# Moving the products of the first half's fourth expert block behind the second half's routing, in a one-layer hybrid decoder

## The chip, the cores and the metric

The kernel runs on one core of one Trainium2 chip. The metric is the device time of one execution in microseconds (us). Three runs of the kernel before took 4314.97, 4318.94 and 4319.62 us; their median, 4318.94 us, is the time before.

## What is computed

One layer on 1024 tokens of width 1024. Three sequence mixers (mLSTM, SSD, forgetting attention) share a normalised input; their outputs are gated, summed and projected with `w_out`. Then comes a product-key expert layer (PEER), and last a gated per-layer embedding and a final norm. The change touches the expert layer:

```
def peer(h, w_q, keys1, keys2, u, v):
    q = (hf @ w_q).astype(f32).reshape(t, PEER_HEADS, 2, PEER_QDIM // 2)
    ...
    v1, i1 = lax.top_k(s1, PEER_TOPK)
    v2, i2 = lax.top_k(s2, PEER_TOPK)
    ...
    gates = jax.nn.softmax(top_s, axis=-1).astype(h.dtype)
    def block(args):
        xb, ib, gb = args
        act = jax.nn.gelu(jnp.einsum('td,thkd->thk', xb, u[ib]), approximate=False)
        return jnp.einsum('thk,thkd->td', act * gb, v[ib])
```

There are 16384 experts, each one row of 1024 fp32 numbers in `u` and one in `v`. Each token picks 8 heads x 16 = 128 experts. For a block of 128 tokens the first `einsum` needs 128 gathers of 128 rows each (one row for each token, 4 KB a row, 512 KB a gather) and 128 row-by-row scalar products.

## The kernel before

The 1024 tokens are worked in two halves of 512, and each half has four blocks of 128 tokens (`tb`). The order of the program is: mixers of half 0, its routing keys (`route_keys`), mixers of half 1 with half 0's routing beside them, then the expert layer, then the embedding.

**Gathers and dots.** `experts_in` (lines 1018 to 1033) handles the first `einsum` of one block. It loads the block's token vectors into the tile `hft`, and for each of the 128 slots `rows` (line 1004) takes a row buffer, POOL issues an indirect DMA into it (line 1014), and VectorE (DVE) multiplies the gathered rows with `hft` and adds along the row (line 1027, in two rows of the trace: the product, named CUSTOM_DVE_ANT_0, and a short read of the accumulator). This document calls the DVE instruction of line 1027 a dot. After the 128th dot ScalarE (ACT) applies the gelu (line 1030) and DVE multiplies with the gates (line 1031).

**Row buffers.** `rows` takes the buffers in turn. `UB = 3` buffers have the tag `ug` in a pool that lives through the program; the argument `extra` adds more. Before the change all four blocks of half 0 get two more, `ug0` and `ug1`, from the mixers' pool (`mx`, in the code `pool["s"]`), so five. A gather into a buffer has to wait until the dot that read its earlier content is done.

**Who decides the order.** Outside of `experts_out` a scheduler of the framework sets each engine's order of instructions: what the program emits earlier goes first where both are ready by its own estimate, and each engine then executes its list strictly in order. The dots of half 0 are emitted after the mixers of half 1 (lines 1341 to 1343) and the scheduler spreads them among those mixers' work.

**What follows the dots.** `mx` is closed (line 1344), and its memory goes to the pool `v1`, with a wait for each tile that overlaps an old one. `scatter` (lines 1059 to 1108) builds one-hot matrices on DVE (lines 1091 and 1103), which PE multiplies in bf16 (line 1070), so that the second `einsum` of three blocks becomes a dense matmul with all of `v`. Its first chunk, for the blocks 0 to 2 of half 0, runs beside `mixer_out(1)`, the projection with `w_out` (lines 876 to 887; its DVE addition is line 884). `route_keys(1)` then starts with a norm: a sum of squares (line 310) and the reciprocal of the root (line 287 is its first DVE row). The routing of half 1 (`route(r1)`, lines 1356 and 1357) is next, and then `experts_out`, where the order on DVE is as written, not scheduled.

Other lines that are named below: 810 normalises the SSD mixer's output, with its statistics in the small operations from line 265 to 226; 840 and 841 combine a branch projection with its gate; 183 makes the low part of a split weight; 205 is an fp32 matmul of a projection; 1347 makes the scatter's `iota` tile, the first DVE row of the scatter.

Of the kernel before, what the change touches and what calls it, by code (L numbers as in the profile page):

```python
# [26 lines left out]
NC = T // P  # L27
# [29 lines left out]
def tile_trunk(ctx, tc, xT, pT, w_in, w_tm, w_br, w_q, keys, peer_u, peer_v,  # L57
# [5 lines left out]
    up = ctx.enter_context(tc.tile_pool(name="up", bufs=1))  # L63
# [10 lines left out]
    def st(shape, dt=F32, tag="t", bufs=1, pool_=None):  # L74
        p = pool_ or pool["r" if tag in ("mg", "rw", "keyt") or tag.startswith("p_") else "s"]
        return p.tile(list(shape), dt, tag=tag, name=nm(tag), bufs=bufs)
# [778 lines left out]
    def mixer(hf, H, columns, side=iter(()), then=None):  # L855
        cd = mg = out = None
        for b, mix in ((2, fox), (0, mlstm), (1, ssd)):
            Y = [ytile() for _ in range(KT)]
            Z = None if hf else halves()
            gs, gate = gates(b, H)  # L860
            if cd is None:
                cd = mix(hf, H, Y, Z, columns, side)
                mg = st([P, KT, T], tag="mg")
                if then is not None:
                    then()
            else:
                mix(hf, H, Y, Z, *cd, gate)
            if b == 1 and hf == 0:
                a = st([P, 4, T], F32R, tag="v8")
                bs = [st([P, 2, T], F32R, tag=f"ug{i}") for i in range(2)]  # L870
                out = [a[:, k] for k in range(4)] + [b_[:, k] for b_ in bs for k in range(2)], []
                out[1].extend(live(dt=F32R) for _ in range(KT))
            branch(gs, gate, b, Z or Y, mg, out)
        return out or mg
# [15 lines left out]
    def top16(src, val, ind, w):  # L890
        V.max(out=val[:, 0:8], in_=src)
        V.max_index(out=ind[:, 0:8], in_max=val[:, 0:8], in_values=src)
        V.match_replace(out=w, in_to_replace=val[:, 0:8], in_values=src, imm_value=-3e38)
        V.max(out=val[:, 8:16], in_=w)
        V.max_index(out=ind[:, 8:16], in_max=val[:, 8:16], in_values=w)
# [35 lines left out]
    def pick(pos, d, ge, gm, starts):  # L931

        V.tensor_tensor(out=ge, in0=pos.unsqueeze(2).to_broadcast([P, 8, 16, 16]),
                        in1=starts.unsqueeze(1).to_broadcast([P, 8, 16, 16]), op=ALU.is_ge)
        o = []
        for x in d:
            V.tensor_tensor(out=gm, in0=ge, in1=x, op=ALU.mult)
            V.tensor_tensor(out=gm[:, :, 0:8], in0=gm[:, :, 0:8], in1=gm[:, :, 8:16], op=ALU.add)
            r = st([P, 8, 16], BF, tag="p_pk", bufs=2 * NC + 1)
            with nc.allow_low_precision(reason="sums of small integers, exact"):  # L940
                V.tensor_reduce(out=r, in_=gm[:, :, 0:8].rearrange("p h a k -> p h k a"), axis=AX.X, op=ALU.add)
            o.append(r)
        return o

    def route(res, tv, ti, ge, gm):

        spare, cs = ge, gm[:, 0:8 * NCAND].rearrange("p (h n) -> p h n", h=8)
        ge, gm = (t.bitcast(BF).rearrange("p (h a k) -> p h a k", h=8, a=16) for t in (ge, gm))
        for tb in range(NC):

            iv = st([P, 16, 17], BF, tag="p_iv")
            V.memset(iv[:, :, 0:1], 0.0)
            V.tensor_copy(out=iv[:, :, 1:17], in_=ti[:, tb])
            dv = st([P, 8, 2, 16], BF, tag="p_dv")
            V.tensor_tensor(out=dv.rearrange("p a b c -> p (a b) c"), in0=iv[:, :, 1:17], in1=iv[:, :, 0:16],
                            op=ALU.subtract)
            vv = tv[:, tb].rearrange("p (a b) c -> p a b c", b=2)
            c0 = 0
            for a, n in CAND:
                V.tensor_tensor(out=cs[:, :, c0:c0 + n], in0=vv[:, :, 1, 0:n],  # L960
                                in1=vv[:, :, 0, a:a + 1].to_broadcast([P, 8, n]), op=ALU.add)
                c0 += n
            V.tensor_tensor(out=cs[:, :, c0:c0 + 8], in0=vv[:, :, 0, 8:16],
                            in1=vv[:, :, 1, 0:1].to_broadcast([P, 8, 8]), op=ALU.add)
            tsc = st([P, 8, 16], tag="p_ts")
            pos = st([P, 8, 16], U32, tag="p_pos")
            for h in range(8):
                top16(cs[:, h, :], tsc[:, h, :], pos[:, h, :], spare[:, h * P:h * P + NCAND])
            posb = st([P, 8, 16], BF, tag="p_pb", bufs=2)
            V.tensor_copy(out=posb, in_=pos)  # L970

            d1 = dv[:, :, 0, :].unsqueeze(3).to_broadcast([P, 8, 16, 16])
            f1, sa = pick(posb, (d1, dst_.unsqueeze(1).to_broadcast([P, 8, 16, 16])), ge, gm, sta)
            bb = st([P, 8, 16], BF, tag="p_pb", bufs=2)
            V.tensor_tensor(out=bb, in0=posb, in1=sa, op=ALU.subtract)
            i1f = f1.rearrange("p h k -> p (h k)")
            d2 = dv[:, :, 1, :].unsqueeze(3).to_broadcast([P, 8, 16, 16])
            f2, = pick(bb, (d2,), ge, gm, stb)
            ii = st([P, P], I32, tag="ii", bufs=NC + 1, pool_=up)
            V.scalar_tensor_tensor(out=ii, in0=i1f, scalar=128.0, in1=f2.rearrange("p h k -> p (h k)"),  # L980
                                   op0=ALU.mult, op1=ALU.add)
            gt = st([P, 8, 16], tag="gt", bufs=2 * NC, pool_=up)
            V.tensor_tensor(out=gt, in0=tsc, in1=tsc[:, :, 0:1].to_broadcast([P, 8, 16]), op=ALU.subtract)
            A.activation(out=gt, in_=gt, func=AF.Exp)
            gsum = st([P, 8], tag="p_gs", bufs=2)
            V.tensor_reduce(out=gsum, in_=gt, axis=AX.X, op=ALU.add)
            V.reciprocal(out=gsum, in_=gsum)
            V.tensor_tensor(out=gt, in0=gt, in1=gsum.unsqueeze(2).to_broadcast([P, 8, 16]), op=ALU.mult)
            res.append([gt, ii, i1f, f2.rearrange("p h k -> p (h k)")])
            yield  # L990

    def route_slots(res, pj=pg):

        for r in res:
            tp = pj((P, 2, P))
            for i in range(2):
                PE.matmul(tp[:, i], lhsT=r[2 + i], rhs=identb, start=True, stop=True)
                t = st([P, P], BF, tag="i12", bufs=4 * NC, pool_=up)
                A.copy(out=t, in_=tp[:, i])
                r[2 + i] = t  # L1000
# [3 lines left out]
    def rows(table, ii, extra):  # L1004

        for s in range(P):
            while True:
                turn["u"] = (turn["u"] + 1) % (len(extra) + UB)
                m = turn["u"]
                p, tag = (up, "ug") if m < UB else extra[m - UB]  # L1010
                if tag not in lent:
                    break
            x = st([P, D], tag=tag, bufs=UB if m < UB else 1, pool_=p)
            G.indirect_dma_start(out=x, out_offset=None, in_=table,  # L1014
                                 in_offset=bass.IndirectOffsetOnAxis(ap=ii[:, s:s + 1], axis=0))
            yield s, x

    def experts_in(hf, tb, r, hpool, extra):


        gt, ii = r[0], r[1]
        gt = gt.rearrange("p a b -> p (a b)")
        act = st([P, P], tag="act", bufs=1, pool_=up)
        hft = st([P, D], tag="hft", bufs=1, pool_=hpool)
        SY.dma_start(out=hft, in_=hfd[hf, tb])
        for s, ug in rows(peer_u, ii, extra):
            V.tensor_tensor_reduce(out=ug, in0=ug, in1=hft, scale=1.0, scalar=0.0,  # L1027
                                   op0=ALU.mult, op1=ALU.add, accum_out=act[:, s:s + 1])
            if s == P - 1:
                A.activation(out=act, in_=act, func=AF.Gelu)  # L1030
                V.tensor_tensor(out=gt, in0=act, in1=gt, op=ALU.mult)
                r.append("weighted")
            yield
# [217 lines left out]
    if True:  # L1251
# [86 lines left out]
        H, c = mixer_head(1)  # L1338
        r0, r1 = [], []
        mg = mixer(1, H, c, route(r0, *k0), lambda: route_slots(r0))  # L1340
    for tb in range(NC):
        for _ in experts_in(0, tb, r0[tb], up, [(pool["s"], "ug0"), (pool["s"], "ug1")]):
            pass
    mx.close()
# [9 lines left out]
    v2, vp = opened("v2", "right")  # L1354
    wa, pool["wa"] = opened("wa", "right")
    for _ in route(r1, *k1):
        pass
    sums = []

# [148 lines left out]
```

## Time and profile before

| what | value |
|---|---|
| median of three runs | 4318.94 us (4314.97 to 4319.62) |
| the profiled execution, its own time | 4315.76 us |
| its span, first to last instruction | 4314.0 us |
| busy in the span | PE 92%, PEld 58%, DVE 76%, POOL 40%, ACT 27% |
| mean granted clock of TensorE | 0.949 of full speed |
| DMA | 1018.30 MB, 236 GB/s over the span |

PE is TensorE's matmuls, PEld its weight loads, DVE VectorE, ACT ScalarE, POOL GpSimd. Times in rows are microseconds from the start of the span. A row of the timeline gives start, duration, engine, line, operation and operands, and in square brackets how long the engine sat idle just before it and what ended that. A row of the windows gives length, then busy time and instruction count of each engine, the granted clock as a share of full speed, the mean busy share of the 16 DMA engines and what they moved in GB/s.

### The profile page before, as it was taken

The numbers are of one execution on the slowest core, as the hardware profiler recorded it, in microseconds if no ns is written. First come the engines' busy times: TensorE is split into PE (matmuls) and PEld (weight loads), VectorE is DVE, ScalarE is ACT, GpSimd is POOL, SyncE is SP. The second block draws the span as 40 slices with busy tenths as digits, with TensorE's granted clock in tenths as the row PEclk, the third lists the DMA queues.
The fourth block names the chain that finished last, engine by engine and source line by source line (L and its number), as shares of the span: only waits on it lengthen the run. The fifth ranks groups of instructions, "written<-read, shape, count | busy, mean of one in ns | idle before, by whom it ended". The sixth has DMA issues, their size and how long they took to land. (4 is left out here: it accounts for less than half of the span.)

```text
span 4314.0 us, 55488 instructions
## 1 busy us (share of the span) xinstructions
PE 3987.3 (92%) x20506; PEld 2494.4 (58%) x20506; DVE 3297.0 (76%) x6607; ACT 1179.5 (27%) x2194; POOL 1726.7 (40%) x1299
## 2 busy tenths in 40 slices
PE   8999999999788988989978798999999999998987
PEld 5777687777466755655744573544445444443455
DVE  6333245648998877788887799998899899997855
ACT  3343334533325502422521410211111111110023
POOL 0000000000036676565364001677777666777620
PEclk9999999999899997899989799999999999999998
DMA  2212122233258898788687124999999999999962
GB/s 91 99 56 76 46 93 71 77 126 122 78 173 296 299 355 291 276 310 313 217 298 282 59 96 149 335 357 361 369 364 376 364 358 361 358 376 400 399 222 93
DMA packets 326081, 1018.30 MB, mean 236 GB/s; under 512 B 33584, under 2 KB 81072, under 8 KB 325552
## 3 DMA queue, kind: packets, MB, share of 16 engines
q0 software_dynamic: 184320, 671.17, 42.6%
q1 hardware_dynamic: 141488, 343.58, 22.5%
q8 instruction: 161, 2.64, 0.2%
q14 instruction: 112, 0.92, 0.1%
HBM read 992.84 MB, written 21.77 MB: 235 GB/s over the span
## 5 line engine op out<-in xcount | busy, mean ns | idle before, releaser
L1014 POOL DMA_INDIRECT ug<-in_peer_u_dram,ii x1024 | 1397.3, 1365 | 2248.3 <-DVE ii L980 1388.6
L1174 PE MATMUL pair<-vr,W 128*128 128x512 f32 x3072 | 1388.7, 603 | 24.5 <-DMA vr<-in_peer_v_dram 24.5
L1027 DVE CUSTOM_DVE_ANT_0 ug<-ug,hft 128x1024 f32<-128x1024 f32 x1024 | 1217.8, 1219 | 158.8 <-DMA ug<-in_peer_u_dram,ii 142.5
L1174 PEld LDWEIGHTS pair<-vr,W 128*128 128x128 f32 x3072 | 569.3, 192 | 661.5 <-issue 633.9
L214 PE MATMUL bank<-hi,wlo 128*128 128x512 f32 x1552 | 623.3, 402 | 24.8 <-DVE wlo L183 24.6
L214 PE MATMUL bank<-hi,whi 128*128 128x512 f32 x1552 | 632.4, 409 | 12.0 <-ACT hi L182 5.1
L214 PE MATMUL bank<-lo,whi 128*128 128x512 f32 x1552 | 624.5, 403 | 0.9 <-DVE lo L183 0.8
L182 ACT CAST whi<-raw 128x1024 fp32r<-128x1024 f32 (+1 forms) x276 | 282.2, 1023 | 1070.9 <-PE bank L214 633.5
L183 DVE TENSOR_TENSOR wlo<-raw,whi 128x1024 fp32r<-128x1024 f32 (+1 forms) x276 | 327.1, 1186 | 323.2 <-ACT whi L182 312.6
L1072 ACT COPY W<-bank 128x176 f32<-128x176 f32 x480 | 179.9, 484 | 950.1 <-PE bank L1070 901.3
L1014 POOL DMA_INDIRECT ug<-in_peer_v_dram,ii x256 | 325.5, 1271 | 184.1 <-DVE hft L1044 95.0
L1044 DVE SCALAR_TENSOR_TENSOR hft<-ug,gt,hft 128x1024 f32<-128x1024 f32 x254 | 325.9, 1283 | 52.8 <-DMA ug<-in_peer_v_dram,ii 47.4
L214 PEld LDWEIGHTS bank<-hi,whi 128*128 128x128 f32 x1552 | 296.0, 191 | 105.3 <-issue 26.4
L214 PEld LDWEIGHTS bank<-hi,wlo 128*128 128x128 f32 x1552 | 296.2, 191 | 102.2 <-DVE wlo L183 32.9
L214 PEld LDWEIGHTS bank<-lo,whi 128*128 128x128 f32 x1552 | 296.4, 191 | 72.4 <-issue 9.7
L1070 PEld LDWEIGHTS <-A 128*128 128x128 bf16 x6912 | 215.2, 98 | 198.7 <-issue 80.9
L1091 DVE TENSOR_TENSOR A<-iota,i 128x1024 bf16<-128x1024 bf16 x288 | 197.4, 686 | 41.8 <-PE bank L1070 36.7
L205 PE MATMUL bank<-Y,raw 128*128 128x512 f32 x384 | 183.4, 636 | 27.8 <-DVE p L840 16.3
L1070 PE MATMUL bank<-Bs,A 128*128 128x43 bf16 (+1 forms) x5760 | 182.3, 183 | 22.4 <-DVE Bs L1103 21.7
L1103 DVE TENSOR_TENSOR Bs<-B,w 128x1032 bf16<-128x1032 bf16 (+1 forms) x288 | 198.4, 689 | 5.9
L205 PEld LDWEIGHTS bank<-Y,raw 128*128 128x128 f32 x384 | 76.6, 203 | 128.5 <-issue 90.3
L329 PE MATMUL pair<-whi,hi 128*128 128x512 f32 x256 | 102.7, 402 | 10.7 <-ACT mg L332 7.6
(429 smaller groups left out, 4492.4 us busy)
## 6 DMA issues: line engine op xcount, KB each, us to landing
vr<-in_peer_v_dram SPq DMA_DIRECT2D x256, 512.0 KB
raw<-in_w_in_dram SPq DMA_DIRECT2D x154, 512.0 KB
raw<-in_w_br_dram SPq DMA_DIRECT2D x64, 512.0 KB
raw<-in_w_tm_dram SPq DMA_DIRECT2D x32, 512.0 KB
raw<-in_w_q_dram SPq DMA_DIRECT2D x32, 512.0 KB
ug<-in_peer_u_dram,ii POOLq DMA_INDIRECT x1024
raw<-in_w_pg_dram SPq DMA_DIRECT2D x14, 512.0 KB
Y<-in_xT_dram SPq DMA_DIRECT2D x16, 256.0 KB
```

The costliest lines, as they stand in the source:

```text
L182: A.copy(out=hi, in_=src)
L183: V.tensor_tensor(out=lo, in0=src, in1=hi, op=ALU.subtract)
L205: PE.matmul(o, lhsT=raw[:, k, :], rhs=X[k] if isinstance(X, list) else X[:, k, :], start=k == 0, stop=k == nk - 1)
L214: PE.matmul(o, lhsT=l[:, k, :], rhs=r[k], start=i == 0, stop=i == n - 1)
L1014: G.indirect_dma_start(out=x, out_offset=None, in_=table, in_offset=bass.IndirectOffsetOnAxis(ap=ii[:, s:s + 1], axis=0))
L1027: V.tensor_tensor_reduce(out=ug, in0=ug, in1=hft, scale=1.0, scalar=0.0, op0=ALU.mult, op1=ALU.add, accum_out=act[:, s:s + 1])
L1044: V.scalar_tensor_tensor(out=o, in0=vg, scalar=gt[:, s:s + 1], in1=o, op0=ALU.mult, op1=ALU.add)
L1070: PE.matmul(wp_[:, u, 0:nk], lhsT=A8[:, a, :, o], rhs=Bs[:, k, a, :, o], start=k == 0, stop=k == 2)
L1072: A.copy(out=W[k][:, 0:hi - lo, b * P + t:b * P + t + 8].rearrange("p i t -> p t i"), in_=wp_[:, :, lo:hi])
L1091: V.tensor_tensor(out=o, in0=iota2[:, k0:k0 + n].unsqueeze(1).to_broadcast([P, 4, n, 2]), in1=x[:, t:t + 8].rearrange("p (a o) -> p a o", ...
L1103: V.tensor_tensor(out=Bs, in0=B8.unsqueeze(1).to_broadcast([P, 3, 4, nk, 2]), in1=w3[:, t // 8].rearrange("p k (a o) -> p k a o", o=2).uns ...
L1174: PE.matmul(acc[b][d], lhsT=l[:, b * P:b * P + P], rhs=raw[:, d * T:d * T + T], start=i2 == 0, stop=i2 == P - 1)
```

## The change

The loop over half 0's blocks runs over three instead of four. The fourth block's `experts_in` is written behind `route(r1, ...)`, and there it gets no extra row buffers (`[]`), since the pool that held `ug0` and `ug1` is closed by then.

```diff
-    for tb in range(NC):
+    for tb in range(3):
         for _ in experts_in(0, tb, r0[tb], up, [(pool["s"], "ug0"), (pool["s"], "ug1")]):
             pass
     mx.close()
...
     for _ in route(r1, *k1):
+        pass
+    for _ in experts_in(0, 3, r0[3], up, []):
         pass
     sums = []
```

The scheduler decides what this does to the order. The two lists, of before and of the change, show it at two places. The first is POOL's queue where the fourth block's gathers begin; `ug0` and `ug1` are the two extra buffers, `ug` the three standing ones. Before:

```order
L1014 DMA ug0_2314_14634<-in_peer_u_dram,ii_1218_8259 128x1024
L1014 DMA ug1_2317_14642<-in_peer_u_dram,ii_1245_8447 128x1024
L1014 DMA ug_2318_14645<-in_peer_u_dram,ii_1245_8447 128x1024
L1014 DMA ug_2319_14648<-in_peer_u_dram,ii_1245_8447 128x1024
L1014 DMA ug_2320_14651<-in_peer_u_dram,ii_1245_8447 128x1024
L1014 DMA ug0_2321_14654<-in_peer_u_dram,ii_1245_8447 128x1024
```

And with the change:

```order
L1014 DMA ug0_2314_14634<-in_peer_u_dram,ii_1218_8259 128x1024
L1014 DMA ug_2654_17731<-in_peer_u_dram,ii_1245_8447 128x1024
L1014 DMA ug_2655_17734<-in_peer_u_dram,ii_1245_8447 128x1024
L1014 DMA ug_2656_17737<-in_peer_u_dram,ii_1245_8447 128x1024
L1014 DMA ug_2657_17740<-in_peer_u_dram,ii_1245_8447 128x1024
L1014 DMA ug_2658_17743<-in_peer_u_dram,ii_1245_8447 128x1024
```

The fourth block's gathers (those with `ii_1245`) stand at the same place of the queue in both, but use three buffers in place of five.

The second place is DVE's list where the scatter begins, beside `mixer_out(1)`. Before:

```order
L1347 COPY iota2_2445_15032<-iotb_4_80 128x256
L884 TENSOR_TENSOR Y_2450_15038<-bank1_67,tmp_2498_15437 128x512
L1027 ISA ug_2443_15020,act_2315_14639<-ug_2443_15020,hft_2316_14640 128x1024
L1027 ISA act_2315_14639 128x1
L1027 ISA ug_2444_15023,act_2315_14639<-ug_2444_15023,hft_2316_14640 128x1024
L1027 ISA act_2315_14639 128x1
L1085 TENSOR_TENSOR wr_2459_15060<-pair0_68,w3_2458_15059 128x128
L1091 TENSOR_TENSOR A8_2460_15065<-iota2_2445_15032,i12_1464_9914 128x1024
```

And with the change:

```order
L1347 COPY iota2_2315_14643<-iotb_4_80 128x256
L1085 TENSOR_TENSOR wr_2329_14671<-pair0_68,w3_2328_14670 128x128
L1091 TENSOR_TENSOR A8_2330_14676<-iota2_2315_14643,i12_1464_9914 128x1024
L1087 TENSOR_TENSOR w3_2328_14670<-wr_2329_14671,w3_2328_14670x8
L1027 ISA ug_2756_18037,act_2652_17728<-ug_2756_18037,hft_2653_17729 128x1024
L1027 ISA act_2652_17728 128x1
L1091 TENSOR_TENSOR B8_2331_14678<-iota2_2315_14643,i12_1465_9917 128x344
L1027 ISA ug_2757_18040,act_2652_17728<-ug_2757_18040,hft_2653_17729 128x1024
L1027 ISA act_2652_17728 128x1
L884 TENSOR_TENSOR Y_2318_14647<-bank1_67,tmp_2326_14655 128x512
```

Before, 126 of the block's 128 dots stand ahead of the scatter's first row (line 1347), and two behind it. With the change 102 stand ahead of it and 26 stand among the scatter's rows and the additions of line 884.

## Rows read from the trace of the kernel before

**Rows 1.** The page's first part: engine, busy us, share of the span, instructions.
```profile
PE 3987.3 (92%) x20506; PEld 2494.4 (58%) x20506; DVE 3297.0 (76%) x6607; ACT 1179.5 (27%) x2194; POOL 1726.7 (40%) x1299
...
L1014 POOL DMA_INDIRECT ug<-in_peer_u_dram,ii x1024 | 1397.3, 1365 | 2248.3 <-DVE ii L980 1388.6
...
L1027 DVE CUSTOM_DVE_ANT_0 ug<-ug,hft 128x1024 f32<-128x1024 f32 x1024 | 1217.8, 1219 | 158.8 <-DMA ug<-in_peer_u_dram,ii 142.5
```

**Rows 2.** Windows: length, PE, PEld, DVE, ACT, POOL busy, granted clock, DMA share, GB/s.
```profile
2156.00:2226.00 70.00, 50.17 (x241) 34.02 (x239) 58.79 (x101) 23.88 (x46) 46.58 (x35) 0.87 0.86 295
2226.00:2326.00 100.00, 90.09 (x227) 44.54 (x228) 78.61 (x132) 4.73 (x6) 64.59 (x51) 0.94 0.89 321
2326.00:2348.00 22.00, 17.08 (x39) 6.87 (x37) 14.70 (x26) 1.99 (x4) 7.45 (x7) 1.00 0.98 374
2348.00:2443.00 95.00, 71.19 (x1194) 47.90 (x1194) 86.85 (x164) 41.82 (x109) 0.00 (x0) 0.75 0.17 56
```

**Rows 3.** Timeline of DVE: milestones between the fourth block's 33rd dot and the norm.
```profile
2156.42 1.21 DVE L1027 CUSTOM_DVE_ANT_0 ug<-ug,hft 128x1024 f32<-128x1024 f32 x1
...
2186.91 1.22 DVE L1027 CUSTOM_DVE_ANT_0 ug<-ug,hft 128x1024 f32<-128x1024 f32 x1
2188.06 0.08 DVE L1027 DVE_READ_ACCUMULATOR2_ANT act<- 128x1 f32 x1
2188.06 1.22 DVE L1027 CUSTOM_DVE_ANT_0 ug<-ug,hft 128x1024 f32<-128x1024 f32 x1
...
2207.41 0.17 DVE L265 TENSOR_SCALAR rw<-pair 128x8 f32<-128x8 f32 x1 [1.09 <-PE pair L252]
...
2224.21 0.68 DVE L226 TENSOR_TENSOR rn<-tmp,tmp 2x512 bf16<-2x512 f32 x1
...
2325.89 0.69 DVE L884 TENSOR_TENSOR Y<-bank,tmp 128x512 f32<-128x512 f32 x1
...
2346.30 1.22 DVE L1027 CUSTOM_DVE_ANT_0 ug<-ug,hft 128x1024 f32<-128x1024 f32 x1 [1.66 <-DMA ug<-in_peer_u_dram,ii]
...
2446.31 0.16 DVE L287 TENSOR_SCALAR rw<-pair 128x4 f32<-128x4 f32 x1 [3.33 <-PE pair L252]
```

**Rows 4.** Waits of 2030 to 2450 us: who waited for whom, us, times, longest.
```profile
ACT w L1084 <- DVE act L1027: 61.1, 1, 61.1
```

**Rows 5.** Line 1027 in 2226 to 2326 us: idle before it, who waited for it.
```profile
  DMA ug<-in_peer_u_dram,ii: 16.3, 13
...
  POOL ug L1014: 26.0, 17
```

**Rows 6.** Timeline of POOL: the 50th, 51st, 52nd, 98th, 117th and 123rd gather of the block.
```profile
2186.66 1.15 POOL L1014 DMA_INDIRECT ug<-in_peer_u_dram,ii  x1 [1.31 <-DVE act L1027]
2188.41 1.68 POOL L1014 DMA_INDIRECT ug<-in_peer_u_dram,ii  x1 [0.60 <-DVE act L1027]
2190.39 1.99 POOL L1014 DMA_INDIRECT ug<-in_peer_u_dram,ii  x1 [0.30 <-issue]
...
2283.81 1.14 POOL L1014 DMA_INDIRECT ug<-in_peer_u_dram,ii  x1 [3.20 <-DVE act L1027]
...
2318.11 0.94 POOL L1014 DMA_INDIRECT ug<-in_peer_u_dram,ii  x1 [0.30 <-issue]
...
2327.09 0.94 POOL L1014 DMA_INDIRECT ug<-in_peer_u_dram,ii  x1 [0.31 <-issue]
```

**Rows 7.** Timeline of DVE: the 50th, 52nd, 98th, 117th and 123rd dot of the block.
```profile
2192.47 1.22 DVE L1027 CUSTOM_DVE_ANT_0 ug<-ug,hft 128x1024 f32<-128x1024 f32 x1 [0.89 <-DMA ug<-in_peer_u_dram,ii]
...
2196.50 1.23 DVE L1027 CUSTOM_DVE_ANT_0 ug<-ug,hft 128x1024 f32<-128x1024 f32 x1 [0.42 <-DMA ug<-in_peer_u_dram,ii]
...
2288.64 1.22 DVE L1027 CUSTOM_DVE_ANT_0 ug<-ug,hft 128x1024 f32<-128x1024 f32 x1
...
2323.45 1.23 DVE L1027 CUSTOM_DVE_ANT_0 ug<-ug,hft 128x1024 f32<-128x1024 f32 x1 [0.15 <-DMA ug<-in_peer_u_dram,ii]
...
2337.21 1.23 DVE L1027 CUSTOM_DVE_ANT_0 ug<-ug,hft 128x1024 f32<-128x1024 f32 x1 [0.66 <-DMA ug<-in_peer_u_dram,ii]
```

## The prediction

> **What bounds the kernel now.** The page gives the whole first: PE is busy for 92% of the span and DVE for 76% [rows 1]. So PE is the engine to watch over the span, but the change acts on one stretch, and that has to be looked at by itself. The windows show it in four pieces [rows 2]. From 2156 to 2326 us the second half's SSD mixer and its branch projections run beside the fourth block's dots: DVE is busy for 58.79 + 78.61 = 137.4 of 170 us, and the DMA engines for 86 to 89%. From 2326 to 2348 us the dots end, at a DMA share of 98%. From 2348 to 2443 us there are no gathers (POOL has no instruction, DMA 17%), DVE is busy for 86.85 of 95 us with the scatter, and PE goes at a mean granted clock of 0.75, a mix of its levels of 1.2 and 2.4 GHz, waiting for the matrices that DVE builds. So two things bound it in turn: the gathers first, DVE later.
>
> That the gathers bind in the first part shows in the waits: in 100 us the dots waited 13 times, 16.3 us in all, for a gather to land, and POOL waited 17 times, 26.0 us, for a dot to free a buffer [rows 5]. Each of the two waits for the other. The scatter could not begin earlier: its first ACT row waited 61.1 us for a dot [rows 4], because its tiles lie in the memory of the mixers' pool, where the last block still used `ug0` and `ug1`.
>
> The milestones are these [rows 3]: the block's 33rd dot starts at 2156.42, the SSD statistics run from 2207.41 (line 265) to 2224.21 (line 226), the first `w_out` addition (line 884) is at 2325.89, the last dot at 2346.30, and the norm's first row (line 287) at 2446.31 after a wait of 3.33 us, so that DVE was through with the scatter at about 2443.
>
> **What the change does.** The text says "behind the routing", the scheduled order says something else. Both DVE lists agree up to the block's 32nd dot, and again from line 287 on, which is the same row in both. In between the dots move back, but not far: ahead of line 265 stand 51 dots in place of 56, ahead of line 226 58 in place of 66, ahead of the first line 884 104 in place of 118, and the last dot stands right behind the seventh of the eight additions of line 884 (before, ahead of the fourth), not behind the routing. No instruction is added or dropped: 1024 dots, 1280 gathers, the same `hft` load on SP's queue at the same place. What is removed is two of five row buffers for this block. What is added is work for DVE to do between the last 24 dots: the scatter, whose memory now comes free with the third block. So the change is worth what these two do to the time of line 287. Behind it the lists agree, and I let the whole shift pass to the end. The few matmuls that change places in the mixers cost nothing: PE has 10 of 100 us idle there [rows 2], which is the cover.
>
> **How fast three buffers turn.** A buffer's turn is: dot, freeing, gather, landing. The 46th dot started at 2186.91 [rows 3] and its buffer's next gather at 2188.41 [rows 6], so 1.50 us from dot to gather. From the gather's start to the dot that waited for it I read, where the dot did wait, 5.81 us (50th: 2186.66 to 2192.47), 6.11 us (52nd: 2190.39 to 2196.50), 5.34 us (117th) and 10.12 us (123rd) [rows 6, 7]; the 98th took 4.83 us and its dot did not wait, so it landed in less. The slow one falls where the DMA engines are 98% busy, at 374 GB/s; the 5.81 and 6.11 where they carry 295 [rows 2]. With three buffers there is less in the air: at 1.96 us a dot (52 dots in the 101.7 us from 2224.21 to 2325.89) the gathers alone carry 0.524 MB / 1.96 us = 268 of 321 GB/s, and at 2.4 us a dot they would carry 218, so 271 in all. That is just under the 295 of the first pair, so I take the lower of the two, 5.8 us. The turn is 5.8 + 1.5 = 7.3 us, and **a dot every 2.43 us**. The bounds are 4.83 us (2.11 us a dot) and, short of the saturated 10.12, some 6.5 us (2.67 us a dot).
>
> The Trainium skill (DMA: Bandwidth & Descriptors, "Anatomy of one DMA — SWDGE (gpsimd) path") fits a DMA issued by GpSimd as 2.0 us plus its bytes at 436 GB/s, which makes an estimated 3.2 us for 512 KB. By that the turn would be 4.7 us, 1.57 us a dot, and three buffers would not bind; no dot here that waited was served as fast, the least being 5.34 us. It is the rival on the faster side, below.
>
> **The sum**, from the 33rd dot on.
> 1. To line 226. 26 dots (58 - 32) x 2.43 = 63.2 us, so 2219.6 in place of 2224.21. The statistics are a chain through PE and ACT too (line 265 waited 1.09 us for PE), so I take a gain of 4 us, not 4.6. Ahead of 2156 the dots stand up to 3 us apart and three buffers keep up; a late gather there meets DVE's idle time.
> 2. From line 226 to the first line 884. 46 dots x 2.43 = 111.8 us in place of 101.7: a loss of 10.1 us. PE was busy for 90 of these 100 us, so it could not take less than about 90 even with all rows at hand.
> 3. From there to the end of the scatter. Before: 2443 - 2325.9 = 117.1 us, of which DVE was busy for 14.70 + 86.85 = 101.6. The change leaves 14 dots more for this part, at 1.15 us each (2186.91 to 2188.06) 16.1 us, and takes about 1.5 us of scatter rows out of it: 116.2 us of work. The last 102 DVE rows are scatter with no dots between; before there were 161 such rows with 8.2 us of idle time (95 - 86.85), so 5.2 us here. The 24 dots among the scatter's rows need 24 x 2.43 = 58 us, and DVE's work there is some 63 us, so the gathers hide, with 2 us for unevenness. 123.4 us, a loss of 6.3 us.
>
> -4 + 10.1 + 6.3 = **+12.4 us at line 287**. The sum stands against the profiled execution, 4315.76 us, which is 3.2 us under the median of 4318.94 us; on the median it gives 4331 us. With 2.11 us a dot: 97.1 us for part 2 (-4.6), no idle time in part 3 (116.2, -0.9), and -4: -9.5 us. With 2.67: part 1 69.4 us (+2, with the chain), part 2 122.8 us (+21), part 3 +7: +30 us.
>
> **The rivals.**
> - *Faster, the other side: the wait for buffers disappears.* One mechanism: with fewer gathers in the air each lands sooner, under 4.8 us from its issue, and DVE fills the remaining gaps with scatter rows, which had 95 us to themselves with PE at a granted clock of 0.75. Its price is part 2 held by PE alone (90 in place of 101.7 us, -11) and part 3 by DVE's work (-1): with part 1's -4, some -14 us, 4305. It decides from 2.0 us a dot downward. For it: in an emptier stretch some gathers were that quick (the 98th). Against it: dots that waited show 5.34 us and more, at five buffers but at no more than 295 GB/s for two of them.
> - *No change.* DVE's work between the two points where the lists agree is the same, 238.9 us of 287. Between 2.0 and 2.3 us a dot parts 1 to 3 sum to within 9 us of nothing: 2.2 us gives -4 - 0.5 + 5 = 0, so 4319.
> - *The dots really stand behind the routing.* Then 128 x 1.15 = 147 us of DVE work would move into a stretch where DVE has nothing to spare, and the time would go up by 100 us or more, less what the mixers gain. The lists speak against it.
>
> **How the numbers follow.** A measurement of this kernel can tell about 0.2%, 8.6 us, from no change. I give the forecast, a turn of 2.3 us or longer, 0.55, no change 0.30, the faster rival 0.13, and the dots behind the routing 0.02. So slower by over 0.2% has 0.57, within it 0.30, faster 0.13. The forecast is 4331 us. The range reaches from 4311, most of the no-change case and the near end of the faster one, to 4349, the +30 of the slow turn.
>
> **What would show it.** Right: the block's dots from the 33rd on are 2.4 us apart up to the first line 884; that line comes some 6 us later than 2325.9 and line 287 some 12 us later than 2446.3; the dots' waits for gathers grow to 30 us or more in the 100 us ahead of line 884, while POOL's rows all wait for dots; the DMA share there falls under 0.85. From line 287 to the end both traces take the same time. Wrong: dots under 2.1 us apart with PE at 95% or more ahead of line 884, a first line 884 ahead of 2316, or a difference that arises behind line 287.

## The result and the profile after

The changed kernel takes 4359.32 us (median of four runs, 4351.86 to 4365.12) beside 4319.28 us for the kernel before: a ratio of 1.0099, 95% interval 1.0085 to 1.0113. It is slower by 40 us, about 1%. The forecast was slower, by 12 us, with a range up to 4349 us: the sign is right, the size is not.

The lines of the page that answer to [rows 1] show as much work as before and more waiting. PE and DVE are busy for the same time within 0.5%; the dots' idle time has grown.

```profile
PE 4006.2 (92%) x20506; PEld 2505.0 (57%) x20506; DVE 3294.8 (76%) x6607; ACT 1179.0 (27%) x2194; POOL 1718.2 (39%) x1299
...
L1014 POOL DMA_INDIRECT ug<-in_peer_u_dram,ii x1024 | 1389.8, 1357 | 2297.3 <-DVE ii L980 1352.3
...
L1027 DVE CUSTOM_DVE_ANT_0 ug<-ug,hft 128x1024 f32<-128x1024 f32 x1024 | 1218.3, 1220 | 195.0 <-DMA ug<-in_peer_u_dram,ii 181.2
```

The dots waited for gathers for 142.5 us over the whole span before, and for 181.2 us now: 38.7 us more. DVE's waits in the stretch between the block's 33rd dot and the norm show that 36.3 us of it are there. The kernel before, in 2156 to 2443 us (columns: us in total, times, longest):

```profile
DVE ug L1027 <- DMA ug<-in_peer_u_dram,ii: 28.5, 27, 3.5
```

The changed kernel, in 2161 to 2482 us:

```profile
DVE ug L1027 <- DMA ug<-in_peer_u_dram,ii: 64.8, 46, 4.5
```

The milestones on DVE's timeline of the changed kernel answer to [rows 3]: the 33rd dot, line 265, line 226, the first addition of line 884, the last dot, and the norm's first row.

```profile
2161.36 1.22 DVE L1027 CUSTOM_DVE_ANT_0 ug<-ug,hft 128x1024 f32<-128x1024 f32 x1
...
2216.91 0.17 DVE L265 TENSOR_SCALAR rw<-pair 128x8 f32<-128x8 f32 x1 [2.45 <-PE pair L252]
...
2232.21 0.68 DVE L226 TENSOR_TENSOR rn<-tmp,tmp 2x512 bf16<-2x512 f32 x1
...
2352.01 0.68 DVE L884 TENSOR_TENSOR Y<-bank,tmp 128x512 f32<-128x512 f32 x1
...
2418.41 1.22 DVE L1027 CUSTOM_DVE_ANT_0 ug<-ug,hft 128x1024 f32<-128x1024 f32 x1
...
2485.35 0.17 DVE L287 TENSOR_SCALAR rw<-pair 128x4 f32<-128x4 f32 x1 [3.33 <-PE pair L252]
```

From the 33rd dot to line 287 it is 324.0 us, before 289.9 [rows 3]: 34.1 us lost, in three pieces. To line 226 70.9 us in place of 67.8, from there to the first line 884 119.8 in place of 101.7, from there to line 287 133.3 in place of 120.4. The windows of these pieces answer to [rows 2]:

```profile
2161.00:2232.00 71.00, 50.25 (x238) 34.69 (x237) 48.12 (x83) 23.79 (x46) 30.26 (x26) 0.91 0.69 228
2232.00:2352.00 120.00, 97.13 (x225) 46.13 (x225) 76.42 (x125) 5.18 (x8) 51.45 (x46) 0.87 0.75 254
2352.00:2421.00 69.00, 58.48 (x511) 29.45 (x509) 58.47 (x111) 16.43 (x41) 25.07 (x22) 0.98 0.81 272
2421.00:2482.00 61.00, 33.46 (x728) 28.69 (x727) 55.63 (x104) 27.16 (x70) 0.00 (x0) 0.58 0.09 32
```

In the second window POOL started 46 gathers in 120 us, one every 2.61 us; before it was 51 in 100, one every 1.96 [rows 2]. The DMA share fell from 0.89 to 0.75 and DVE's busy time from 79 of 100 to 76 of 120 us. PE was busy for 97 of 120 us at a granted clock of 0.87, before for 90 of 100 at 0.94. Nothing is full there any more: DVE and the DMA engines each wait for the other.

The profiled execution lost 49 us, of which 39 by line 287 (34 in the stretch, 5 ahead of its 33rd dot). Those 5 us are not shown to come from the change: the 33rd dot starts at 2161.4 us here and at 2156.4 before, but at 2148.4 in a run below that has the order and the buffers of the kernel before up to there, and at 2151.3 in one with three buffers. The other 10 us are lost at the end. From the last of the 3072 matmuls of line 1174 to the end of the span it took 195.8 us (4167.55 to 4363.36), before 184.5 (4129.46 to 4313.99). This document calls that the last part. ACT's copies of the finished sums (line 1135) show where the two begin to differ. Before, on ACT's timeline:

```profile
4126.65 1.07 ACT L1135 COPY es<-pair 128x512 f32<-128x512 f32 x2 [35.42 <-PE pair L1174]
4128.37 1.07 ACT L1135 COPY es<-pair 128x512 f32<-128x512 f32 x2 [0.64 <-PE pair L1174]
4130.08 1.07 ACT L1135 COPY es<-pair 128x512 f32<-128x512 f32 x2 [0.64 <-PE pair L1174]
```

With the change:

```profile
4170.99 3.03 ACT L1135 COPY es<-pair 128x512 f32<-128x512 f32 x6 [41.68 <-DVE hft L1044]
```

Before, the copies follow PE, and the first starts 2.8 us ahead of the last matmul. Now all six wait for a DVE instruction of line 1044, which adds up gathered rows of `v` and still reads one of their buffers. They end 6.5 us after the start of the last matmul in place of 1.7; that is 4.8 of the 11.3 us, and where the rest goes stays open. The counter `turn["u"]` that hands out row buffers has run modulo 3 instead of 5 for 128 slots, and so, by the code of `rows`, stands at 2 in place of 1 when the second half's blocks begin. From then on each gather meets another buffer than before.

### The profile page after: what moved, and what is told of

It is laid out like the page before. It is cut to its first block, busy times and chain, and to the rows that moved or that the text cites. A ratio compares the mean times of both kernels' runs of the same rounds, so it can differ in the third digit from the quotient of the medians.

```text
span 4363.4 us, 55487 instructions
## 1 busy us (share of the span) xinstructions
PE 4006.2 (92%) x20506; PEld 2505.0 (57%) x20506; DVE 3294.8 (76%) x6607; ACT 1179.0 (27%) x2194; POOL 1718.2 (39%) x1299
## 5 line engine op out<-in xcount | busy, mean ns | idle before, releaser
L1027 DVE CUSTOM_DVE_ANT_0 ug<-ug,hft 128x1024 f32<-128x1024 f32 x1024 | 1218.3, 1220 | 195.0 <-DMA ug<-in_peer_u_dram,ii 181.2
L214 PE MATMUL bank<-hi,wlo 128*128 128x512 f32 x1552 | 624.1, 403 | 27.9 <-DVE wlo L183 27.8
L1070 PE MATMUL bank<-Bs,A 128*128 128x43 bf16 (+1 forms) x5760 | 182.6, 183 | 21.7 <-DVE Bs L1103 20.9
```

Source lines behind the costliest of these rows:

```text
L214: PE.matmul(o, lhsT=l[:, k, :], rhs=r[k], start=i == 0, stop=i == n - 1)
L1070: PE.matmul(wp_[:, u, 0:nk], lhsT=A8[:, a, :, o], rhs=Bs[:, k, a, :, o], start=k == 0, stop=k == 2)
```

## The experiments

Theory "buffers": the loss is DVE standing still for gathers because three buffers turn too slowly. Rival "place": it comes from where the dots now stand, among the scatter and `mixer_out`. A side question is the counter. The kernel before, run beside each group of experiments, had medians of 4316.43, 4314.94 and 4315.49 us; the ratios stand against those.

**Three buffers at the old place.**

```diff
-        for _ in experts_in(0, tb, r0[tb], up, [(pool["s"], "ug0"), (pool["s"], "ug1")]):
+        for _ in experts_in(0, tb, r0[tb], up, [(pool["s"], "ug0"), (pool["s"], "ug1")] if tb < 3 else []):
```

> The kernel before, with one edit: the fourth block keeps its place in the program but gets no extra row buffers, so three in place of five. Theory 'buffers' (the loss is DVE standing still for gathers because three buffers turn too slowly, wherever the dots are written): the dots between line 226 and the first line 884 are about 2.6 us apart as in the changed kernel, DVE's waits for gathers from the block's 33rd dot on are some 60 us in place of 28.5, line 287 comes at 2475 to 2490 us, and the time is 4345 to 4365 us. Theory 'place' (the loss comes from the dots standing among the scatter's rows and the additions of line 884): most dots are again ahead of the scatter here, so at most 12 us are lost, 4319 to 4331 us.

Measured 4370.2 us, ratio 1.0123 (1.0102 to 1.0144): slower than the change itself, and 5 us over the range given for "buffers". DVE's waits in 2155 to 2480 us:

```profile
DVE ug L1027 <- DMA ug<-in_peer_u_dram,ii: 73.7, 50, 3.7
```

The two ends of the stretch on DVE's timeline, the 33rd dot and line 287:

```profile
2151.31 1.22 DVE L1027 CUSTOM_DVE_ANT_0 ug<-ug,hft 128x1024 f32<-128x1024 f32 x1
...
2490.19 0.17 DVE L287 TENSOR_SCALAR rw<-pair 128x4 f32<-128x4 f32 x1 [3.33 <-PE pair L252]
```

The stretch takes 338.9 us, and ahead of the first line 884 a dot comes every 2.60 us, as with the change. The old place saves nothing. "Buffers" holds, "place" falls: where the dots stand even helps a little with three buffers (324.0 beside 338.9 us). In this run 14 dots stand between the first and the second addition of line 884, in the changed kernel four; scatter rows stand among them in both. The counter is at 2 here too, and the last part is 193.8 us.

**Four buffers at the new place, and the control of its layout.** The second extra buffer moves from the mixers' pool to the standing pool `cp` under the tag `xg`, so that it outlives `mx`; the later pool `vp` gives one of its five and uses `xg` instead, and the index tiles are four instead of five.

```diff
-    for _ in experts_in(0, 3, r0[3], up, []):
+    for _ in experts_in(0, 3, r0[3], up, [(cp, "xg")]):
...
-        ex = [(vp, f"ug{i}") for i in range(5)]
+        ex = [(vp, f"ug{i}") for i in range(4)] + [(cp, "xg")]
```

> The changed kernel with four row buffers for the fourth block: one of the two extra buffers is moved from the mixers' pool to a standing pool (paid for by one index tile and one buffer of the later pool, so that every other block keeps its count of buffers). The dots stay where the change puts them. Theory 'buffers': a turn of about 8.2 us over four buffers is 2.05 us a dot, near the 1.99 of before, so most of the loss comes back: 4319 to 4335 us. Theory 'place': the place is the same as in the changed kernel, so 4345 to 4360 us.

> The kernel before with the memory layout of the four-buffer run (one extra buffer standing, one index tile fewer), five buffers and the old place for the fourth block. Both theories: as before, 4314 to 4326 us. Any other time is the price of the layout and has to be taken off the four-buffer run.

The control took 4313.63 us, ratio 0.9991 (0.9978 to 1.0003): the layout costs nothing. Four buffers at the new place took 4326.11 us, ratio 1.0019 (1.0004 to 1.0034), so 0.8 of the change's 1.0% is back. Not all of that is the buffer's: modulo 4 the counter comes to stand at 3 and not at 2, and the last part is 181.4 us in place of 195.8. Its two ends of the stretch:

```profile
2148.35 1.22 DVE L1027 CUSTOM_DVE_ANT_0 ug<-ug,hft 128x1024 f32<-128x1024 f32 x1
...
2447.52 0.17 DVE L287 TENSOR_SCALAR rw<-pair 128x4 f32<-128x4 f32 x1 [3.33 <-PE pair L252]
```

299.2 us, so 24.8 of the 34.1 us lost in the stretch are back, with a dot every 2.17 us ahead of the first line 884, against 2.05 expected.

**Four buffers at the old place.** The layout control, with `[tb // 3:]` behind its list of the two extra buffers.

> The layout control with four in place of five row buffers for the fourth block, at the old place. With the four runs so far this fills the table of three, four and five buffers at the old place (five: control 4313.6, three: 4370) beside three and four at the new one (4359, 4326). Theory 'buffers alone': place is worth nothing, so the time is that of four buffers moved, 4320 to 4330 us. Theory 'buffers, and the new place gives some back' (with three, the old place was 11 us slower than the new one): 4328 to 4342 us, a dot still every 2.2 us ahead of the first line 884.

4328.88 us, ratio 1.0032 (1.0018 to 1.0045); the stretch takes 306.6 us:

```profile
2158.58 1.22 DVE L1027 CUSTOM_DVE_ANT_0 ug<-ug,hft 128x1024 f32<-128x1024 f32 x1
...
2465.18 0.17 DVE L287 TENSOR_SCALAR rw<-pair 128x4 f32<-128x4 f32 x1 [3.33 <-PE pair L252]
```

In the stretch the new place is better by 7.4 us with four buffers, while runs that differ in the counter alone agree there within 4 us (table below). Of the whole time that shows as 0.13%, with intervals that overlap, so what the place is worth in the end stays open at that size.

**A quarter of the gathers.** In `rows` only every fourth slot of the fourth block issues a gather, and four dots in turn use its tile. Left out are 96 of the block's 128 gathers; all dots stay, so most of them multiply what an earlier dot left in the tile.

```diff
         for s in range(P):
+            if s % every:
+                yield s, x
+                continue
             while True:
```

> The changed kernel, but the fourth block gathers only every fourth of its 128 slots, and each gathered tile is used by four dots in turn, so 96 gathers are left out and all 128 dots stay. It takes away the wait for row buffers without touching DVE's work. Theory 'buffers': DVE's waits for these gathers nearly vanish, the time falls to 4290 to 4315 us, within 8 us of the same cut in the kernel before. Theory 'place': the dots among the scatter's rows cost time by themselves, and it stays 20 us or more above that control.

> The kernel before with the same cut: the fourth block gathers every fourth slot, five buffers, the old place. Control for the run before it. Both theories: 4285 to 4312 us, as the 28.5 us of DVE's waits for this block's gathers go and the DMA engines have less to do.

The new place took 4284.25 us (0.9924, 0.9909 to 0.9940), the old one 4271.94 us (0.9898, 0.9882 to 0.9913). Both are faster than expected, by 6 and 13 us beyond the ranges. The dots' waits are gone from DVE's list in both. The ends of the stretch, at the new place (lines 1027 and below stand three lines lower in these two kernels):

```profile
2157.65 1.22 DVE L1030 CUSTOM_DVE_ANT_0 ug<-ug,hft 128x1024 f32<-128x1024 f32 x1
...
2409.94 0.17 DVE L287 TENSOR_SCALAR rw<-pair 128x4 f32<-128x4 f32 x1 [3.33 <-PE pair L252]
```

And at the old one:

```profile
2151.39 1.22 DVE L1030 CUSTOM_DVE_ANT_0 ug<-ug,hft 128x1024 f32<-128x1024 f32 x1
...
2404.20 0.17 DVE L287 TENSOR_SCALAR rw<-pair 128x4 f32<-128x4 f32 x1 [3.33 <-PE pair L252]
```

252.3 and 252.8 us: without the gathers' limit the place of the dots is worth nothing in the stretch, either way. The 12 us between the two runs are more than the 8 that "buffers" allowed. The profiled ones are 14 us apart: 10.8 us lie in the last part, 188.9 beside 178.1 us, and go with the counter, which stands at 2 in the one and at 0 in the other; no run sets it back here. Another 6.3 us lie ahead of the 33rd dot, where kernels of one order differ as much.

**The counter.** `turn["u"] = 1` is set ahead of the second half's blocks: in the changed kernel, then in the one with four buffers. And in the kernel before, `turn["u"] = 2`, the change's value, and nothing else.

> The changed kernel, with the counter that hands out row buffers set back, before the second half's blocks, to the value it had there in the kernel before. The four runs of the changed kernel lie at 4352 to 4365 us; its profiled one loses 39 us up to the second half's norm and 10 us more in the last 200 us, where the last gathers wait for a lent buffer. Theory 'rotation' (those 10 us come from the last gathers meeting other buffers than before): the last part is as long as before and the time is 4350 to 4357 us in all runs. Theory 'chance' (the last part differs from run to run by itself): the runs spread over 4352 to 4365 us as those of the change do.

> Four buffers at the new place, as in the four-buffer run (4326), and the counter of row buffers set back ahead of the second half's blocks as in the run that restored it (12 us less there). Theory 'rotation': the last part, from the last matmul with the rows of v to the end, is about 182 us as before, and it was 181 in the four-buffer run already, so nothing is gained: 4318 to 4330 us. If the counter is worth something by itself: 4308 to 4316 us, under the kernel before.

> The kernel before, and only the counter of row buffers set, ahead of the second half's blocks, to the value that the change leaves there. Nothing else of the change. Theory 'rotation': ACT's last copies of the dense products wait for a dot that still holds their buffer, as in the changed kernel, the stretch from the last matmul with the rows of v to the end is 192 to 196 us in place of 184.5, and the time is 8 to 12 us over the kernel before, 4323 to 4328 us beside 4315. Theory 'chance': within 4 us of the kernel before.

The changed kernel with the counter set back took 4347.59 us, ratio 1.0063 (1.0046 to 1.0080), 0.36% less than the change. Its four runs lie at 4338 to 4365 us, lower and wider than the 4350 to 4357 expected. Its copies follow PE again:

```profile
4177.48 1.07 ACT L1135 COPY es<-pair 128x512 f32<-128x512 f32 x2 [34.97 <-PE pair L1174]
```

and the last part is 182.7 us. Its profiled run lost 9 us elsewhere, between the first and the last matmuls of line 1174, which I can't explain. The kernel before with the change's counter took 4323.22 us, ratio 1.0022 (1.0007 to 1.0038), and its copies wait as in the change:

```profile
4130.42 3.03 ACT L1135 COPY es<-pair 128x512 f32<-128x512 f32 x6 [41.82 <-DVE hft L1044]
```

So the counter alone costs 0.2%, some 8 us. The size agrees with what was expected; the place only in part, since the last part of its profiled run grew by 3.4 us to 187.9, not to 192. All four runs with the counter at 2 have the six copies in one wait and a last part of 188 to 196 us; in the eight others it is 178 to 185 us. The run with four buffers and the counter set took 4319.69 us (1.0013, 1.0003 to 1.0023) beside 1.0019 without: no difference beyond the intervals. With the counter at 1 in both, the fourth buffer at the new place is worth 4347.59 - 4319.69 = 27.9 us.

**Six buffers.** The kernel before, with a third extra buffer in the mixers' pool for all four blocks. The memory comes from fewer index tiles, lists and small tiles; `turn["u"] = 1` keeps the counter.

```diff
-    iot = st([P, P], I32, tag="ii", bufs=NC + 1, pool_=up)
+    iot = st([P, P], I32, tag="ii", bufs=NC, pool_=up)
...
-                t = st([P, P], BF, tag="i12", bufs=4 * NC, pool_=up)
+                t = st([P, P], BF, tag="i12", bufs=3 * NC, pool_=up)
...
-        pool["small"] = pool["r"], 6, "rw"
+        pool["small"] = pool["r"], 5, "rw"
...
-        ... [(pool["s"], "ug0"), (pool["s"], "ug1")]):
+        ... [(pool["s"], "ug0"), (pool["s"], "ug1"), (pool["s"], "ug2")]):
```

> The kernel before with six row buffers for the four blocks of the first half (a third extra one in the mixers' pool; its memory comes from four index tiles, one list of slots and one small statistics tile that have no reader waiting), the counter ahead of the second half as in the kernel before. Theory 'buffers': the same relation as three, four and five go on, with less to win since the DMA engines are 86 to 98% busy there: from the block's 33rd dot to line 287 some 280 to 288 us in place of 290, and 4295 to 4312 us in all. Rival 'bandwidth': at five buffers the DMA engines bind and not the buffers, so 4311 to 4320 us.

4255.81 us, ratio 0.9869 (0.9845 to 0.9892): 1.3% faster than the kernel before, and the fastest kernel here with the full computation. The gain is three times the most that was expected. The fourth block's stretch takes 280.2 us, at the near end of what was said:

```profile
2100.99 1.21 DVE L1027 CUSTOM_DVE_ANT_0 ug<-ug,hft 128x1024 f32<-128x1024 f32 x1
...
2381.18 0.17 DVE L287 TENSOR_SCALAR rw<-pair 128x4 f32<-128x4 f32 x1 [3.33 <-PE pair L252]
```

But the block's first dot comes at 1992.9 in place of 2052.2 us. I had counted the fourth block alone, and the three before it wait for the same buffers. The dots' idle time in 1170 to 2480 us, before:

```profile
  DMA ug<-in_peer_u_dram,ii: 130.1, 124
```

With six buffers:

```profile
  DMA ug<-in_peer_u_dram,ii: 58.9, 65
```

No run has these smaller tiles with five buffers. That the whole gain is the sixth buffer's is argued from the waits, which fell by 71 us, and not shown.

All runs, sorted by the stretch from the block's 33rd dot to line 287; the counter is what `turn["u"]` holds when the second half's blocks begin, by the code:

| place | buffers | counter | stretch, us | last part, us | ratio to before |
|---|---|---|---|---|---|
| old | three | 2 | 338.9 | 193.8 | 1.0123 |
| new (the change) | three | 2 | 324.0 | 195.8 | 1.0099 |
| new | three | 1 | 323.7 | 182.7 | 1.0063 |
| old | four | 3 | 306.6 | 182.6 | 1.0032 |
| new | four | 3 | 299.2 | 181.4 | 1.0019 |
| new | four | 1 | 298.1 | 182.1 | 1.0013 |
| old | five | 2 | 293.6 | 187.9 | 1.0022 |
| old (layout control) | five | 1 | 292.3 | 182.8 | 0.9991 |
| old (before) | five | 1 | 289.9 | 184.5 | 1 |
| old | six | 1 | 280.2 | 184.6 | 0.9869 (all four blocks) |
| old, quarter of the gathers | five | 0 | 252.8 | 178.1 | 0.9898 |
| new, quarter of the gathers | three | 2 | 252.3 | 188.9 | 0.9924 |

## Why the prediction was right in its sign and wrong in its size

**Right.** The change does not put the dots behind the routing; it takes two of five buffers from a block whose gathers bind, and the loss is DVE waiting for rows. Two marks given for that came: the dots' waits ahead of line 884 grew from 16.3 [rows 5] to 41.4 us, and the DMA share fell to 0.75. A third came for the most part: of POOL's 46 gathers there 32 waited for a dot, not all. This is line 1027 in 2232 to 2352 us:

```profile
  DMA ug<-in_peer_u_dram,ii: 41.4, 29
...
  POOL ug L1014: 61.5, 32
```

DVE's work in the stretch is the same, as said: 48.12 + 76.42 + 58.47 + 55.63 = 238.6 us, 238.9 forecast.

**The term that was mis-sized** is the turn, "5.8 + 1.5 = 7.3 us". It was some 7.85 us (a dot every 2.61 us, three buffers), though the dots that waited were served faster than I took it. The timeline of two gathers on POOL in the changed kernel, the block's 70th and 76th:

```profile
2258.61 1.04 POOL L1014 DMA_INDIRECT ug<-in_peer_u_dram,ii  x1 [0.30 <-issue]
...
2277.22 0.94 POOL L1014 DMA_INDIRECT ug<-in_peer_u_dram,ii  x1 [0.30 <-issue]
```

and of their dots on DVE:

```profile
2266.18 1.22 DVE L1027 CUSTOM_DVE_ANT_0 ug<-ug,hft 128x1024 f32<-128x1024 f32 x1
...
2283.19 1.23 DVE L1027 CUSTOM_DVE_ANT_0 ug<-ug,hft 128x1024 f32<-128x1024 f32 x1 [1.14 <-DMA ug<-in_peer_u_dram,ii]
```

The 76th dot waited, and took its rows 5.97 us after the gather's start; the 70th did not wait, and still came 7.57 us after it. So its rows lay in the buffer while DVE did something else or waited for an earlier gather. Between line 226 and the first line 884, 29 of 46 dots waited, with a median of 5.39 us from gather to dot, but the mean over all 46 is 6.15 us, and 1.70 us from a dot to the next gather. An estimate from the DMA packets in the trace, counted off in the order of the gathers, splits the 6.15 us: the last packet of a gather ended 5.2 us after its start on the mean (before, 6.0 us), and the dot came 1.0 us behind that. I had put the landing into the turn and left out the time that a landed buffer waits for an engine that works strictly in order. The rows before could have told: five buffers at 1.96 us a dot make a turn of 9.8 us, where two latencies picked out had given 7.3. By the Trainium skill's fit (DMA: Bandwidth & Descriptors, "Anatomy of one DMA — SWDGE (gpsimd) path") the landing would be an estimated 3.2 us; the fastest of the 29 took 4.36 us, so the trace does not agree, as it did not before.

The other terms: part 1 was given as a gain of 4 us and was a loss of 3.1, since line 226 is reached at the same slow turn (26 gathers in the 71 us of the first window, 2.7 us each) and the chain did not wait less (line 265 waited 2.45 us for PE, before 1.09). Part 2 was a loss of 18.1, given as 10.1. Part 3 was 12.9, given as 6.3: the gathers among the scatter's rows did not hide; the dots waited 10.2 us there, where I had allowed 2. The turn alone does not carry the time out of the range: with 2.61 us a dot the prediction's own sum gives 0 + 18.4 + 6.3, some 25 us at line 287, where 34.1 us were lost in the stretch.

**The step that failed outright** is "I let the whole shift pass to the end". The lists of DVE agree behind line 287, but the buffers that the instructions name do not: the counter had moved, and that cost some 8 to 12 us more (8 in the kernel before, 12 in the change, by the medians). The prediction had named "a difference that arises behind line 287" as a sign of being wrong, and it came. I had looked at the order alone. No term of the sum stood for it.

Of the rivals, "the wait for buffers disappears" fell with the 41.4 us of waits, though its premise held, that rows land sooner with fewer gathers in the air (6.0 to 5.2 us by the estimate above), "no change" with the result, and the dots did not go behind the routing.

## What to carry to other kernels

Before a tile is given fewer buffers, divide its whole turn by their count, and take for the turn the mean over all uses in the trace, not the latency of those that waited: on an engine that works in order a landed buffer waits too. Where two engines each show waits for the other over a ring of buffers, try one buffer more before taking the transfers' engines for the limit, even at 86 to 89% busy: here the run with one more was 1.3% faster. And a counter that hands out buffers is part of an edit: the same order with other buffers behind it is another program.

## What was not expected of the hardware

At 86 to 98% of the DMA engines' time [rows 2] I took the gathers to be near their limit of bandwidth. With six buffers the share in 1500 to 1800 us went only from 0.87 to 0.90 and the rate from 310 to 324 GB/s, and yet the dots' waits fell by 71 us: the buffers had bound, not the bandwidth. The window before:

```profile
1500.00:1800.00 300.00, 262.51 (x938) 167.53 (x937) 229.75 (x388) 71.05 (x107) 187.55 (x144) 0.85 0.87 310
```

And with six buffers:

```profile
1500.00:1800.00 300.00, 276.25 (x1053) 180.14 (x1052) 242.24 (x416) 82.22 (x125) 202.61 (x152) 0.86 0.90 324
```

Runs of one kernel spread over 0.7% here (the kernel before from 4297 to 4328 us over all groups), more than the 0.2% that I had set as what can be told.
